# A one-core Mamba-2, attention and ConvFFN trunk: the low halves of the in-projection's weights are subtracted on GpSimd, and 22 small parameter loads are issued behind the first two of them

## The chip, the cores and the metric

The kernel runs on one core of a Trainium2 chip. The metric is the device time of one execution in microseconds; three runs of the kernel before gave a median of 1357.01 us. The core has five engines that take instructions from queues of their own, each in program order: TensorE (PE, matrix products; PEld is its loading of weights), VectorE (DVE), ScalarE (ACT), GpSimd (POOL) and SyncE (SP, here only the issuing of transfers). GpSimd and ScalarE can issue transfers too. Engines wait for each other through semaphores.

## The reference

For a sequence of 512 tokens of width 1024 (float32) the reference computes two layers. Only the first stage of the first layer matters here:

```python
def mamba2_mixer(x, ln_g, in_w, conv_w, conv_b, dt_bias, a_log, d_skip, norm_g, out_w):
    zxbcdt = rms_norm(x, ln_g) @ in_w
    z, xbc, dt = ...
    xbc = jax.nn.silu(causal_dwconv(xbc, conv_w, conv_b))
    ...
    dt = jax.nn.softplus(dt + dt_bias)
    a = dt * (-jnp.exp(a_log))
    y = ssd_chunked(xs32 * dt[..., None], a, bm, cm)
    y = y + xs32 * d_skip[:, None]
    y = y.reshape(b, s, D_INNER) * jax.nn.silu(z)
    y = rms_norm(y in 4 groups, norm_g)
    return y @ out_w
```

The in-projection `in_w` is 1024 wide on the input side and has 5152 columns: 2048 for `z`, 2048 for `x`, 512 for `B`, 512 for `C` and 32 for `dt`. After the mixer come a ConvFFN, a shared key/value projection, differential attention and a second ConvFFN.

## The kernel before, in words

**Products.** The stream is held transposed, 128 features on the partitions and 512 tokens along them. TensorE multiplies numbers of a shortened float32 type (fp32r). To keep float32 accuracy each operand is a sum of a high part (the value rounded to fp32r) and a low part (what is left over), and each product is three: high weights by high stream, high weights by low stream, low weights by high stream (`mm3`, lines 195 to 198). A block of 128 output columns of the in-projection takes 8 steps along its 1024 inputs, so 24 products of 128x512.

**Weights.** All weights pass in one order, the list `plan`: `dt` (32 columns), then for each of four groups one `B` block (`in32` to `in35`), one `C` block (`in36` to `in39`), four `x` blocks (`in16` and up) and four `z` blocks (`in0` and up), then the out-projection of the group before. Every entry is a chunk of 128x1024 numbers, 512 KB. The class `Weights` takes a chunk in three steps: SyncE loads it into one of three buffers `wr`; ScalarE copies it, rounded, into `wh` (`high`, line 147); VectorE subtracts `wh` from `wr` and writes `wl` (`low`, line 151). `wh` and `wl` have three buffers each. A chunk is taken two ahead of its use (`AHEAD`), so a `high` waits until the chunk three places earlier has been used up. There are 40 chunks of the in-projection. `in32` and `in36` (`c0`, `c1_`) are written out by hand ahead of the loop, 38 go through `split`.

**Start.** While the input is transposed and split into `xgh` and `xgl`, GpSimd issues the loads of all small parameters: first those needed soon, then 22 that are needed late (lines 259 to 272): `k_norm_g`, `q_norm_g`, `subln_g` and `lam_vecs` into the tile `s2t`, and 16 pieces of the ConvFFN's kernels and biases into `sf`. TensorE reads `s2t` through one transpose and `sf` through four (`pst`, line 235).

**The decay chain.** The first products give `dt` for all tokens. It is turned to lie along the tokens (`al_x`, line 456, and `ps_dtt`, line 550), then VectorE takes some twenty short steps on 128x128 numbers (`dt`, `sp_p`, `sp_s`, lines 558 to 577) up to `A`. TensorE sums `A` along a chunk of tokens (`ps_dec`, lines 581 to 583). The sums go out to memory and back, spread over the partitions (`cumd`, line 602; `m`, line 623; `er`, line 628; all issued by GpSimd), GpSimd sets what lies above the diagonal of `m` to minus infinity (line 633), ScalarE takes the exponential, and the scan's products (`st`, `y`, `yo`) use it. Between those steps VectorE runs the convolution of every `x`, `B` and `C` block (`ctmp`, line 535, three steps each), the `z` blocks' scaling and the scan's element-wise work.

**What orders the work.** Each engine's queue is filled by a scheduler that orders the instructions by their dependences and their expected length; a call inside `pin` is held in the order in which the program makes it. GpSimd has little to do: parameter loads, the transfers and selects of the scan, and a few sums of squares (`gacc`, line 785; `nacc`, line 499).

Of the kernel before, what the change touches and what calls it, by code (L numbers as in the profile page):

```python
# [18 lines left out]
P = 128  # L19
# [9 lines left out]
FFN = 2816  # L29
# [10 lines left out]
def trunk_kernel(ctx: ExitStack, tc, x, ssm_ln_g, ssm_in_w, ssm_conv_w, ssm_conv_b, ssm_dt_bias,  # L40
# [4 lines left out]
    act, dve, pool, pe, sync = nc.scalar, nc.vector, nc.gpsimd, nc.tensor, nc.sync  # L45
# [80 lines left out]
    pin = tc.keep_in_program_order  # L126

    class Weights:
# [17 lines left out]
            self.wl = wp.tile([P, 1024], F32R, tag="wl", name="wl_" + self.key)  # L146
            return act.activation(self.wh[:, :self.n], self.raw[:, :self.n], AF.Copy)  # L147

        def low(self):
            ready.append((self.key, self.cols(self.wh), self.cols(self.wl)))  # L150
            return dve.tensor_tensor(out=self.wl[:, :self.n], in0=self.raw[:, :self.n],  # L151
                                     in1=self.wh[:, :self.n].bitcast(F32), op=ALU.subtract)

        def split(self):
            if self.gcol is None:
                self.high()
                self.low()
                return

            wh = self.wh = wp.tile([P, 1024], F32R, tag="wh", name="wh_" + self.key)  # L160
            wl = self.wl = wp.tile([P, 1024], F32R, tag="wl", name="wl_" + self.key)
            for k in range(self.nk):
                ks = slice(k * self.ncol, (k + 1) * self.ncol)
                g = c2[:, self.gcol + k:self.gcol + k + 1]
                act.activation(wh[:, ks], self.raw[:, ks], AF.Copy, scale=g)
                dve.scalar_tensor_tensor(out=wl[:, ks], in0=self.raw[:, ks], scalar=g,
                                         in1=wh[:, ks].bitcast(F32), op0=ALU.mult, op1=ALU.subtract)
            ready.append((self.key, self.cols(wh), self.cols(wl)))
# [10 lines left out]
    pin = tc.keep_in_program_order  # L179
# [49 lines left out]
    sf = bp.tile([P, 4, P], F32, tag="nsq", name="sf", bufs=2)  # L229
    s2t = bp.tile([P, T], F32, tag="nsq", name="s2t", bufs=2)  # L230
    st2, lamv, d2 = s2t[:80, 0:P], s2t[:, P:3 * P].rearrange("p (a b) -> p a b", a=4), s2t[:, 384:386]
# [6 lines left out]
    with tc.tile_pool(name="ph0", bufs=1) as p0:  # L238
# [17 lines left out]
        pin(pool.dma_start(st2[16:32, :], ffn_ln_g.rearrange("o (b p) -> (o b) p", p=P)))  # L256
        pin(pool.dma_start(st2[32:40, :], kv_ln_g.rearrange("(b p) -> b p", p=P)))
        pin(pool.dma_start(st2[40:48, :], attn_ln_g.rearrange("o (b p) -> (o b) p", p=P)))
        for j in range(2):
            pin(pool.dma_start(st2[48:49, j * 64:(j + 1) * 64], k_norm_g.unsqueeze(0)))  # L260
            pin(pool.dma_start(st2[49:50, j * 64:(j + 1) * 64], q_norm_g))
        pin(pool.dma_start(st2[50:51, :], subln_g))
        pin(pool.dma_start(lamv.rearrange("p a b -> p (a b)"),
                       lam_vecs.rearrange("o a b -> (o a b)").partition_broadcast(P)))
        for l in range(2):
            for j in range(2):
                cols = slice(j * FFN, (j + 1) * FFN)
                d = sf[:, 2 * l + j, :]
                for t in range(3):
                    pin(pool.dma_start(d[22 * t:22 * (t + 1), :],  # L270
                                   ffn_conv_w[l, t, cols].rearrange("(b p) -> b p", p=P)))
                pin(pool.dma_start(d[66:88, :], ffn_conv_b[l, cols].rearrange("(b p) -> b p", p=P)))


        warm = aux_bank("warm")
        for _ in range(10):
# [36 lines left out]
        c0 = Weights(1)  # L313
        square(1)
        square(2)
        c1_ = Weights(2, xt[3])
        pss = [(mm_bank if k >= 4 else aux_bank)("xgt%d" % k) for k in range(6)]
        for b in range(NT):
            for k in range(6):
                turn(b, k)  # L320
        high(0)
        low(0)
        wdt = cdt.both()
        high(1)
        low(1)
        high(2)
        keep(0)
        keep(1)
        low(2)
        pss.extend(aux_bank("xgt%d" % k) for k in range(6, KB))  # L330
        ps_dt, ps_b0 = mm_bank("ps_dt"), mm_bank("ps_in32")
# [23 lines left out]
        for k in range(4, 6):  # L355
            high(k)
            low(k)
        pin(c0.low())
        for k in range(6, KB):
            high(k)  # L360
            low(k)
        pin(c1_.high())
        pin(c1_.low())
        state["next"], state["use"] = 3, 1
        square(3)
        for k in (4, 5, 2, 3, 6, 7):
# [150 lines left out]
    with tc.tile_pool(name="ssm_y", bufs=1) as yp, tc.tile_pool(name="ssm", bufs=1) as sp:  # L517
# [74 lines left out]
        ncum = sp.tile([P, P], F32, name="ncum")  # L592
        dve.tensor_scalar(out=ncum, in0=ps[:, P:2 * P], scalar1=-1.0, scalar2=None, op0=ALU.mult)
        dve.tensor_copy(rows(cum[:, 0, :]), split(ps[:, P:2 * P]))
        dve.tensor_copy(rows(cum[:, 1, :]), split(dec[:, P:2 * P]))
        ps = aux_bank("ps_cum")
        cumT = sp.tile([P, 2, P], F32, name="cumT")
# [611 lines left out]
```

## Time and profile before

| quantity | value |
|---|---|
| median of three runs (lowest, highest) | 1357.01 us (1356.84, 1357.68) |
| the profiled execution | 1357.51 us |
| its span in the profile | 1355.3 us |
| TensorE busy, instructions | 99%, 6421 |
| VectorE busy, instructions | 68%, 1527 |
| ScalarE busy, instructions | 48%, 1066 |
| GpSimd busy, instructions | 7%, 118 |
| granted TensorE clock | full in every slice |

The span runs from the first to the last instruction; 2.2 us of the execution lie around it. A row of a timeline gives the start (in us from the span's start), the duration, the engine, the line of the kernel, the operation, the tile that is written and those that are read, and in brackets how long the engine stood idle before and what ended that. Several alike in a row are one row with a count. A product's shown duration is longer than its distance to the next, since products overlap in the array; it is the distance that counts.

### The profile page before, as it was taken

The numbers are of one execution on the slowest core, as the hardware profiler recorded it, in microseconds if no ns is written. First come the engines' busy times: TensorE is split into PE (matmuls) and PEld (weight loads), VectorE is DVE, ScalarE is ACT, GpSimd is POOL, SyncE is SP. The second block draws the span as 40 slices with busy tenths as digits, with TensorE's granted clock in tenths as the row PEclk, the third lists the DMA queues.
The fourth block names the chain that finished last, engine by engine and source line by source line (L and its number), as shares of the span: only waits on it lengthen the run. The fifth ranks groups of instructions, "written<-read, shape, count | busy, mean of one in ns | idle before, by whom it ended". The sixth has DMA issues, their size and how long they took to land.

```text
span 1355.3 us, 16860 instructions
## 1 busy us (share of the span) xinstructions
PE 1348.1 (99%) x6421; PEld 1096.3 (81%) x6421; DVE 917.8 (68%) x1527; ACT 653.9 (48%) x1066; POOL 88.4 (7%) x118
## 2 busy tenths in 40 slices
PE   9999999999999999999999999999999999999998
PEld 7877887887888888888888777777888888888887
DVE  5989888688887774267754555778777773367742
ACT  5696744652444442234433556767654442134420
POOL 4230300200010000000001000000110000000000
PEclk9999999999999999999999999999999999999999
DMA  7452433532333333333323422221223333333322
GB/s 203 144 164 78 148 109 94 148 94 70 94 93 94 94 95 104 97 94 94 101 78 107 124 84 85 77 76 37 78 84 90 104 95 94 93 101 102 94 93 78
DMA packets 179904, 135.06 MB, mean 100 GB/s; under 512 B 6508, under 2 KB 163632, under 8 KB 179824
## 3 DMA queue, kind: packets, MB, share of 16 engines
q1 hardware_dynamic: 174048, 120.84, 30.0%
q0 software_dynamic: 4496, 12.05, 2.9%
q8 instruction: 50, 0.82, 0.3%
q10 hardware_dynamic: 1280, 1.10, 0.2%
q14 instruction: 30, 0.25, 0.1%
HBM read 131.72 MB, written 2.25 MB: 99 GB/s over the span
## 4 chain that ended last, share of the span: by engine, by line
PE 95%; DVE 3%; ACT 1%; issue 1%; DMA 0%; POOL 0%; SPq 0%; DVEq 0%; ACTq 0%
PE ps_g L197 6%; PE ps_g L198 6%; PE ps_g L196 6%; PE ps_u L198 6%; PE ps_u L196 6%; PE ps_u L197 6%; PE ps_in L197 5%; PE ps_in L196 5%; PE ps_in L198 5%; PE ps_d L854 3%; PE ps_d L198 3%; PE ps_d L197 3%; PE ps_d L853 3%; PE ps_d L852 3%; PE ps_d L196 3%; PE ps_o L196 2%
## 5 line engine op out<-in xcount | busy, mean ns | idle before, releaser
L196 PE MATMUL ps_u<-xgh,wh_u 128*128 128x512 f32 x352 | 137.4, 390 | 0.0
L197 PE MATMUL ps_g<-xgl,wh_g 128*128 128x512 f32 x352 | 137.2, 390 | 0.0
L196 PE MATMUL ps_g<-xgh,wh_g 128*128 128x512 f32 x352 | 137.0, 389 | 0.0
L198 PE MATMUL ps_u<-xgh,wl_u 128*128 128x512 f32 x352 | 137.0, 389 | 0.0
L198 PE MATMUL ps_g<-xgh,wl_g 128*128 128x512 f32 x352 | 137.0, 389 | 0.0
L197 PE MATMUL ps_u<-xgl,wh_u 128*128 128x512 f32 x352 | 136.9, 389 | 0.0
L197 PE MATMUL ps_in<-xgl,wh_in 128*128 128x512 f32 x304 | 120.9, 398 | 0.0
L196 PE MATMUL ps_in<-xgh,wh_in 128*128 128x512 f32 x304 | 120.9, 398 | 0.0
L151 DVE TENSOR_TENSOR wl_d<-wr_d,wh_d 128x1024 fp32r<-128x1024 f32 (+1 forms) x46 | 54.2, 1179 | 96.9 <-ACT wh_d L147 96.7
L198 PE MATMUL ps_in<-xgh,wl_in 128*128 128x512 f32 x304 | 119.6, 393 | 0.0
L147 ACT ACTIVATE wh_d<-wr_d 128x1024 fp32r<-128x1024 f32 (+1 forms) x46 | 47.1, 1024 | 130.6 <-PE ps_d L854 62.4
L876 ACT ACTIVATE hh<-vg 128x512 fp32r<-128x512 f32 x44 | 27.8, 632 | 114.9 <-DVE vg L875 114.9
L824 DVE TENSOR_TENSOR uu<-ps_u,nr_f 128x512 f32<-128x512 f32 x44 | 30.4, 692 | 78.0 <-PE ps_u L198 77.8
L197 PEld LDWEIGHTS ps_g<-xgl,wh_g 128*128 128x128 f32 x352 | 66.1, 188 | 14.5 <-DVE xgl L414 0.7
L198 PEld LDWEIGHTS ps_u<-xgh,wl_u 128*128 128x128 f32 x352 | 66.0, 188 | 13.8
L196 PEld LDWEIGHTS ps_u<-xgh,wh_u 128*128 128x128 f32 x352 | 66.2, 188 | 13.5
L198 PEld LDWEIGHTS ps_g<-xgh,wl_g 128*128 128x128 f32 x352 | 66.1, 188 | 13.5
L197 PEld LDWEIGHTS ps_u<-xgl,wh_u 128*128 128x128 f32 x352 | 66.0, 188 | 13.6
L196 PEld LDWEIGHTS ps_g<-xgh,wh_g 128*128 128x128 f32 x352 | 66.0, 187 | 13.6
L147 ACT ACTIVATE wh_g<-wr_g 128x1024 fp32r<-128x1024 f32 x44 | 46.7, 1061 | 50.5 <-PE ps_u L197 32.2
L196 PE MATMUL ps_d<-hh,wh_d 128*128 128x512 f32 x176 | 68.5, 389 | 0.0
L197 PE MATMUL ps_d<-hl,wh_d 128*128 128x512 f32 x176 | 68.5, 389 | 0.0
(347 smaller groups left out, 3178.3 us busy)
## 6 DMA issues: line engine op xcount, KB each, us to landing
wr_g<-in_ffn_up_w_dram SPq DMA_DIRECT2D x44, 512.0 KB, 3.8
wr_u<-in_ffn_up_w_dram SPq DMA_DIRECT2D x44, 512.0 KB, 3.8
wr_d<-in_ffn_down_w_dram SPq DMA_DIRECT2D x42, 512.0 KB, 3.6
wr_in<-in_ssm_in_w_dram SPq DMA_DIRECT2D x40, 512.0 KB, 3.9
m<-cumd POOLq DMA_DIRECT2D x16, 512.0 KB, 4.5
wr_out<-in_ssm_out_w_dram SPq DMA_DIRECT2D x16, 512.0 KB, 3.5
wr_k<-in_kv_w_dram SPq DMA_DIRECT2D x8, 512.0 KB, 3.8
wr_q<-in_q_w_dram SPq DMA_DIRECT2D x8, 512.0 KB, 3.8
```

Of the source, the lines that this page charges most:

```text
L147: return act.activation(self.wh[:, :self.n], self.raw[:, :self.n], AF.Copy)
L151: return dve.tensor_tensor(out=self.wl[:, :self.n], in0=self.raw[:, :self.n], in1=self.wh[:, :self.n].bitcast(F32), op=ALU.subtract)
L196: pe.matmul(ps, wh, xh, start=start, stop=False)
L197: pe.matmul(ps, wh, xl, start=False, stop=False)
L198: return pe.matmul(ps, wl, xh, start=False, stop=stop).ins
L824: dve.tensor_tensor(out=u, in0=ps, in1=r, op=ALU.mult)
L852: pe.matmul(pss[b], hh[k][:, ts], wh[:, k - k0, :], start=k == 0, stop=False)
L853: pe.matmul(pss[b], hh[k][:, ts], wl[:, k - k0, :], start=False, stop=False)
L854: pe.matmul(pss[b], hl[k][:, ts], wh[:, k - k0, :], start=False, stop=k == n - 1)
L876: act.activation(h, ga, AF.Copy)
```

## The change

`low` takes the engine as an argument. The low parts of all 40 chunks of the in-projection, 128x1024 each, are subtracted on GpSimd; those of all other weights stay on VectorE. The 22 late parameter loads move from their place ahead of the first products to a place behind the low part of `in36`.

```diff
-        def low(self):
+        def low(self, eng=dve):
             ready.append((self.key, self.cols(self.wh), self.cols(self.wl)))
-            return dve.tensor_tensor(out=self.wl[:, :self.n], in0=self.raw[:, :self.n],
+            return eng.tensor_tensor(out=self.wl[:, :self.n], in0=self.raw[:, :self.n],
                                      in1=self.wh[:, :self.n].bitcast(F32), op=ALU.subtract)
         def split(self):
             if self.gcol is None:
                 self.high()
-                self.low()
+                self.low(pool if self.key[:2] == "in" else dve)
                 return
...
         pin(pool.dma_start(st2[40:48, :], attn_ln_g.rearrange("o (b p) -> (o b) p", p=P)))
-        for j in range(2):
-            pin(pool.dma_start(st2[48:49, j * 64:(j + 1) * 64], k_norm_g.unsqueeze(0)))
...
-                pin(pool.dma_start(d[66:88, :], ffn_conv_b[l, cols].rearrange("(b p) -> b p", p=P)))
...
-        pin(c0.low())
+        pin(c0.low(pool))
         for k in range(6, KB):
             high(k)
             low(k)
         pin(c1_.high())
-        pin(c1_.low())
+        pin(c1_.low(pool))
+        for j in range(2):
+            pin(pool.dma_start(st2[48:49, j * 64:(j + 1) * 64], k_norm_g.unsqueeze(0)))
...
+                pin(pool.dma_start(d[66:88, :], ffn_conv_b[l, cols].rearrange("(b p) -> b p", p=P)))
```

The 14 lines that move are the same in both places. What GpSimd's queue holds behind the last of these loads, before the change (a name's first part is the tile, `x3` means three alike in a row):

```order
L270 DMA sf_112<-in_ffn_conv_w_dram 22x128 x3
L272 DMA sf_112<-in_ffn_conv_b_dram 22x128
L602 DMA cumd0_417<-cumT_416 128x128
L602 DMA cumd1_418<-cumT_416 128x128
L623 DMA m0_0_429<-cumd0_417 128x1024
```

And after it, at the same place of GpSimd's queue:

```order
L360 DMA sf_112<-in_ffn_conv_w_dram 22x128 x3
L362 DMA sf_112<-in_ffn_conv_b_dram 22x128
L151 TENSOR_TENSOR wl_in16_449<-wr_in16_446,wh_in16_448 128x1024
L151 TENSOR_TENSOR wl_in17_463<-wr_in17_460,wh_in17_462 128x1024
L151 TENSOR_TENSOR wl_in18_483<-wr_in18_480,wh_in18_482 128x1024
L151 TENSOR_TENSOR wl_in19_522<-wr_in19_519,wh_in19_521 128x1024
L151 TENSOR_TENSOR wl_in0_572<-wr_in0_569,wh_in0_571 128x1024
L151 TENSOR_TENSOR wl_in1_622<-wr_in1_619,wh_in1_621 128x1024
L601 DMA cumd0_417<-cumT_416 128x128
L601 DMA cumd1_418<-cumT_416 128x128
L622 DMA m0_0_429<-cumd0_417 128x1024
```

Six subtractions, of the four `x` blocks and the first two `z` blocks of group 0, now stand between the late loads and the transfers of the decay chain. The subtractions of `in2` and `in3` follow behind the four selects of group 0, those of the later groups in the same way.

Since the scheduler orders what is not pinned, TensorE's queue changes as well. Before, the block `in16` begins in the usual pattern of three, right behind the transpose of `st1`, the last instruction of the hand-written start:

```order
L383 MATMUL pst_339<-ident_77,st1_122 128x120
L196 MATMUL ps_in16_486<-xgh0_86,wh_in16_448 128x512
L197 MATMUL ps_in16_486<-xgl0_94,wh_in16_448 128x512
L198 MATMUL ps_in16_486<-xgh0_86,wl_in16_449 128x512
L196 MATMUL ps_in16_486<-xgh1_87,wh_in16_448 128x512
L197 MATMUL ps_in16_486<-xgl1_95,wh_in16_448 128x512
```

After the change:

```order
L382 MATMUL pst_339<-ident_77,st1_122 128x120
L196 MATMUL ps_in16_486<-xgh0_86,wh_in16_448 128x512
L197 MATMUL ps_in16_486<-xgl0_94,wh_in16_448 128x512
L196 MATMUL ps_in17_525<-xgh0_86,wh_in17_462 128x512
L197 MATMUL ps_in17_525<-xgl0_94,wh_in17_462 128x512
L455 MATMUL al_x_364<-ident_77,rs_84 128x128 x4
L549 MATMUL ps_dtt_372<-ident_77,dtT_370 128x64 x4
L198 MATMUL ps_in16_486<-xgh0_86,wl_in16_449 128x512
L196 MATMUL ps_in16_486<-xgh1_87,wh_in16_448 128x512
```

Two products of `in17` and the eight transposes of `al_x` and `ps_dtt` now stand ahead of the first product that reads the low part of `in16`. The three products of `ps_dec` move as well. Before, they stand in the block `in19`:

```order
L197 MATMUL ps_in19_625<-xgl5_99,wh_in19_521 128x512
L581 MATMUL ps_dec_404<-A_401,lt_81 128x128
L582 MATMUL ps_dec_404<-A_401,ut_79 128x128
L583 MATMUL ps_dec_404<-A_401,ones_75 128x128
L198 MATMUL ps_in19_625<-xgh5_91,wl_in19_522 128x512
```

After it they stand in `in18`, at the same step of the block:

```order
L197 MATMUL ps_in18_575<-xgl5_99,wh_in18_482 128x512
L580 MATMUL ps_dec_404<-A_401,lt_81 128x128
L581 MATMUL ps_dec_404<-A_401,ut_79 128x128
L582 MATMUL ps_dec_404<-A_401,ones_75 128x128
L198 MATMUL ps_in18_575<-xgh5_91,wl_in18_483 128x512
```

That is one block of 24 products earlier. The scan's products of group 0 that follow stand earlier by about as much.

More of the change, by code (lines that the diff above doesn't have):

```diff
@@ L258, in trunk_kernel @@
         pin(pool.dma_start(st2[40:48, :], attn_ln_g.rearrange("o (b p) -> (o b) p", p=P)))
-        for j in range(2):
[L260 to L272, printed above, removed]
         warm = aux_bank("warm")
@@ L362, in trunk_kernel @@
         pin(c1_.high())
-        pin(c1_.low())
+        pin(c1_.low(pool))
+        for j in range(2):
+            pin(pool.dma_start(st2[48:49, j * 64:(j + 1) * 64], k_norm_g.unsqueeze(0)))
+            pin(pool.dma_start(st2[49:50, j * 64:(j + 1) * 64], q_norm_g))
+        pin(pool.dma_start(st2[50:51, :], subln_g))
+        pin(pool.dma_start(lamv.rearrange("p a b -> p (a b)"),
+                       lam_vecs.rearrange("o a b -> (o a b)").partition_broadcast(P)))
+        for l in range(2):
+            for j in range(2):
+                cols = slice(j * FFN, (j + 1) * FFN)
+                d = sf[:, 2 * l + j, :]
+                for t in range(3):
+                    pin(pool.dma_start(d[22 * t:22 * (t + 1), :],
+                                   ffn_conv_w[l, t, cols].rearrange("(b p) -> b p", p=P)))
+                pin(pool.dma_start(d[66:88, :], ffn_conv_b[l, cols].rearrange("(b p) -> b p", p=P)))
         state["next"], state["use"] = 3, 1
```

## The prediction

> **What bounds the kernel now.** I read the page's busy times first, then the chain that ended last, then TensorE's waits.
>
> ```profile
> PE 1348.1 (99%) x6421; PEld 1096.3 (81%) x6421; DVE 917.8 (68%) x1527; ACT 653.9 (48%) x1066; POOL 88.4 (7%) x118
> PE 95%; DVE 3%; ACT 1%; issue 1%; DMA 0%; POOL 0%; SPq 0%; DVEq 0%; ACTq 0%
> ```
>
> TensorE carries the chain. Its waits (waiting line, releaser: total us, count, longest) say how little another engine could give back:
>
> ```profile
> PE warm L277 <- DVE ones L202: 1.1, 1, 1.1
> PE tr_g L446 <- DVE gacc L785: 0.4, 1, 0.4
> PE at L1050 <- DVE lg L1042: 0.4, 1, 0.4
> PE st L675 <- DVE xe L658: 0.3, 1, 0.3
> ```
>
> Behind the warm-up nothing waits longer than 0.4 us. VectorE's relief, however large, can buy about 0.7 us (`tr_g` and `st`) where it is relieved. The relief is 48.9 us of work that nothing waited for (the group's row is below), so the question is whether TensorE gets new waits. A product costs what lies between two starts:
>
> ```profile
> 27.32 0.39 PE L197 MATMUL ps_in<-xgl,wh_in 128*128 128x512 f32 x1
> 27.55 0.40 PE L198 MATMUL ps_in<-xgh,wl_in 128*128 128x512 f32 x1
> ...
> 31.06 0.62 PE L456 MATMUL al_x<-ident,rs 128*128 128x128 f32 x4
> 31.61 0.46 PE L550 MATMUL ps_dtt<-ident,dtT 64*128 64x64 f32 x4
> 32.00 0.50 PE L197 MATMUL ps_in<-xgl,wh_in 128*128 128x512 f32 x1
> ```
>
> 27.55 - 27.32 = 0.23 us a 512-wide product; `al_x` and `ps_dtt` together take 32.00 - 31.06 = 0.94. The row at 27.55 is the first product that reads the low part of `in16`.
>
> **What one subtraction costs on GpSimd.** The first row is the group that leaves VectorE; GpSimd subtracts nothing so far, and the nearest rows are its 512-wide additions, with VectorE's 512-wide addition as the last row:
>
> ```profile
> L151 DVE TENSOR_TENSOR wl_in<-wr_in,wh_in 128x1024 fp32r<-128x1024 f32 x40 | 48.9, 1223 | 3.8 <-ACT wh_in L147 3.8
> 369.15 1.29 POOL L499 TENSOR_TENSOR nacc_f<-nacc_f,nsq_f 128x512 f32<-128x512 f32 x1 [30.55 <-ACT nsq_f L497]
> 373.01 1.30 POOL L499 TENSOR_TENSOR nacc_f<-nacc_f,nsq_f 128x512 f32<-128x512 f32 x1 [2.57 <-ACT nsq_f L497]
> 369.12 1.87 DVE L414 SCALAR_TENSOR_TENSOR xgl<-xT,c,xgh 128x512 fp32r<-128x512 f32 x1
> ...
> 373.05 0.68 DVE L511 TENSOR_TENSOR xT<-ps_o,xT 128x512 f32<-128x512 f32 x1
> ```
>
> Twice 1.29 gives 2.58; scaled as VectorE scales, 1.29 x 1.22 / 0.68, it is 2.3. I take 2.4. The loads behind it and the next step of GpSimd's queue:
>
> ```profile
> 11.71 0.50 POOL L260 DMA_DIRECT2D s2t<-in_k_norm_g_dram  x1
> ...
> 25.06 0.51 POOL L272 DMA_DIRECT2D sf<-in_ffn_conv_b_dram  x1
> 53.47 0.57 POOL L602 DMA_DIRECT2D cumd<-cumT  x1 [27.91 <-issue]
> ...
> 68.06 1.09 POOL L633 TENSOR_SCALAR_AFFINE_SELECT m<-m 128x1024 f32<-128x1024 f32 x1 [2.74 <-DMA m<-cumd]
> ```
>
> The 22 issues took 25.57 - 11.71 = 13.9 us with their pauses, and need at least 22 x 0.51 = 11.2.
>
> **The first two blocks: free.** ScalarE's high part of `in36`, and the first products that read the low parts of `in32` and `in36`:
>
> ```profile
> 15.36 1.12 ACT L147 ACTIVATE wh_in<-wr_in 128x1024 fp32r<-128x1024 f32 x1
> 19.72 1.98 PE L375 MATMUL ps_in<-xgh,wl_in 128*128 128x512 f32 x8
> 21.99 0.39 PE L381 MATMUL ps_in<-xgh,wl_in 128*128 128x512 f32 x1
> ```
>
> On GpSimd `in36` is done at 15.36 + 1.12 + 2.4 = 18.9, three us before its use, and `in32`, whose high part came earlier, by 17.8. The moved parameters are issued by 32.8 at the latest (term 1) and are first read within the decay chain, some microseconds behind that, so their own lateness costs nothing; reloading the raw buffers stays hidden too, since a block of 24 products lasts 24 x 0.23 = 5.5 us.
>
> **Term 1, `in16`.** Its subtraction now stands behind the 22 issues: from 18.9 they last until 30.1 (11.2) to 32.8 (13.9). I take 31.0, towards the lower end, because the rows of the single issues are the nearest to what is asked; plus 2.4 gives 33.4 (32.5 to 35.3). Nothing else on GpSimd is late by that: what is queued behind are the other subtractions, whose blocks come later. TensorE reaches its first use two products of `in17` and the transposes later than before: 27.55 + 2 x 0.23 + 0.94 = 28.95. The wait is 4.5 us (3.5 to 6.3). Part of it would come anyway, since `al_x` needs `rs`:
>
> ```profile
> 28.04 1.23 DVE L151 TENSOR_TENSOR wl_in<-wr_in,wh_in 128x1024 fp32r<-128x1024 f32 x1
> ...
> 30.75 0.16 DVE L429 SCALAR_TENSOR_TENSOR rs<-rst_x,rs 128x4 f32<-128x4 f32 x1
> 32.10 0.29 DVE L558 COPY dt<-ps_dtt 128x128 f32<-128x128 f32 x1 [1.20 <-PE ps_dtt L550]
> ...
> 48.00 0.28 DVE L577 SCALAR_TENSOR_TENSOR A<-dt,alog 128x128 f32<-128x128 f32 x1
> ```
>
> `rs` was ready at 30.91; without the subtraction in its midst it is at 29.8, against 28.0 for TensorE at `al_x`. That is 1.8 us, inside the 4.5.
>
> **Term 2, `ps_dec`.** It stands one block earlier:
>
> ```profile
> 48.68 0.39 PE L581 MATMUL ps_dec<-A,lt 128*128 128x128 f32 x2
> 65.69 0.39 PE L198 MATMUL ps_in<-xgh,wl_in 128*128 128x512 f32 x1
> L535 DVE SCALAR_TENSOR_TENSOR ctmp<-u,c,ctmp 128x511 f32<-128x511 f32 x24 | 17.7, 743 | 0.0
> ```
>
> TensorE comes there 61 products behind the first use of `in16`'s low part: 33.4 + 61 x 0.23 = 47.4. VectorE's chain to `A` took 48.28 - 32.10 = 16.2 us. Two subtractions (2.4) and one convolution step (0.74) fall out of it: 13.0. It starts at 29.8 + 0.94 = 30.7, so `A` is there at 43.7, in time, if VectorE runs as fast as before. But the rows at 369 show that it doesn't: beside GpSimd's addition `xgl` took 1.87 us, against 0.74 of the alike step in the `L535` row, so it stood for 1.13 of GpSimd's 1.29, 88%. The addition out of PSUM at 373.05 was not slowed. Five subtractions (`in16` to `in0`) fall into this chain: 12.0 us, less some 2.4 in which VectorE reads PSUM, times 0.88, is 8.4. `A` then comes at 52.1, and TensorE waits 4.7 us (0 to 5.9). It is an estimate from one pair of rows; the chain's steps have two inputs outside PSUM, as `xgl` had, so I take that row.
>
> The Trainium skill, page "GPSIMD Engine Reference", section "8. Key points", says that GpSimd shares its SBUF interfaces with VectorE and contends with VectorE's instructions that have two SBUF inputs. For `xgl` the trace agrees, with 1.87 against 0.74; for convolution steps no run here shows it. By that rule term 2 stays as it is; without it, it would be nought.
>
> **Term 3, `in2`.** Its subtraction stands behind the transfers and selects of group 0. `A` at 52.1 would put the first of these transfers at 52.1 + (53.47 - 48.28) = 57.3. Ahead of it on GpSimd now stands the subtraction of `in1`, whose high part waits until `in18` is used up: 52.1 + 0.4 for `ps_dec` + 7 x 0.23 + 1.1 (a high part) + 2.4 = 57.6, which decides by a little. The last select follows 14.6 us later as before, at 72.2; with its 1.1 and 2.4 more, the low part is there at 75.7. TensorE needs it at 65.69 before; less 0.94 and 0.46 that have moved ahead of `in16` and 0.3 of a moved scan product, 36.4 us behind `in16`'s first use: 33.4 + 36.4 + 4.7 = 74.5. The wait is 1.2 (0 to 3).
>
> **Term 4, groups 1 to 3.** There 30 subtractions meet a VectorE that is in places full:
>
> ```profile
> 120.00:150.00 30.00, 30.00 (x183) 23.09 (x182) 29.35 (x47) 17.03 (x31) 4.80 (x7) 1.00 0.40 127
> ```
>
> (The window, its length, then the busy time of PE, PEld, DVE, ACT and POOL with counts, TensorE's granted clock and the transfers' share and rate.) VectorE is busy for 29.35 of 30 us in the scan, whose order has changed. For each subtraction of 1.22 that it loses it can stand for up to 2.1 (0.88 x 2.4), so it comes out up to 0.9 later for each, and behind it are queued the scan's steps on which TensorE's `st`, `y` and `yo` wait. GpSimd itself, busy for 4.80 of the 30, has room for these. I take 1.5 us over three groups (-0.7, the relief above, to 5).
>
> **Sum.** 4.5 + 4.7 + 1.2 + 1.5 = 11.9. The profiled run took 1357.51, 1355.3 of it the span; the median is 1357.01, and the terms are differences, so I add them to the median: 1368.9.
>
> **Rivals.**
>
> *The port doesn't bite the chain (A).* For: only one kind of step was seen slowed, and a 128x128 step may slip between. Against: 88% at `xgl`. Then term 2 is gone and term 3 with it, and 4.5 + 1.5 + some 1 for a partly slowed chain makes 1364. Chance 0.20.
>
> *TensorE's clock falls in the pauses (C).* The warm-up shows what a cold clock costs:
>
> ```profile
> 1.13 4.63 PE L277 MATMUL warm<-ones 128*128 128x128 f32 x20 [1.13 <-DVE ones L202]
> ...
> 9.40 1.28 PE L344 MATMUL ps_in<-ones 128*128 128x128 f32 x10
> ```
>
> 4.63 / 20 = 0.23 a product at the start, 1.28 / 10 = 0.13 later: about half speed, for between 4.6 us (the first row alone) and 8.3 (until the second). Half of that is lost, 2.3 to 4.1 a fall. No pause of before is long enough to show whether 4.5 us suffice. One or both pauses falling add about 3: 1371.9. Chance 0.19.
>
> The Trainium skill, page "TensorE: Matmul & The Clock Gate", Part 1, says that one idle window of about 3.4 us halves the clock and that about 3.4 busy us restore it. By that figure a fall would lose an estimated 1.7 us, and the forecast with two falls would be 1372.3; no run here shows a fall within the kernel.
>
> *Not slower (B).* This needs the late loads off `in16`'s way: all 22 issued by 28.95 - 2.4 = 26.5, in 7.6 us instead of 11.2, that is at 0.35 each or on fewer instructions than the order shows, and the port free. Then the pause on `rs`, 1.8, less the relief, 0.7, is left: 1358.1. Nothing in the rows speaks for issues that short. Chance 0.06.
>
> **How the numbers follow.** The forecast has the remaining 0.55. Its bounds with small terms (3.5 + 1 + 0) and A reach down to 1361; C with term 1 at its upper end and two or three us more in the later groups reaches 1377. That leaves out B and little at either end, some 0.15. A measurement of this kernel tells about 0.2%, 2.7 us, from no change: faster by more 0.01, within 0.05 (B), slower 0.94.
>
> **What would show it.** Term 1: GpSimd's 22 issues in one row until about 31, `wl_in16` until 33, TensorE's longest wait on it, near 4.5 us. Term 2: a wait of `ps_dec` on `A`, and convolution steps well over 0.74 us wherever a subtraction runs. Term 3: a small wait in `in2`. C: slower products behind a pause, or a granted clock under 1. I am wrong if the `in16` wait is under 2 us, if the steps of the decay chain keep their 0.28 us beside GpSimd, or if a later group holds a wait larger than these.

## The result and the profile after

Five runs of the changed kernel gave a median of 1403.95 us (1399.96 to 1405.26), beside 1357.01 of the kernel before on the same chip: a ratio of 1.0339 (95% interval 1.0327 to 1.0351), 46.9 us slower, where 11.9 us were forecast. The profiled execution took 1403.95 us, with a span of 1402.2.

The page of the changed kernel, busy times:

```profile
PE 1359.3 (97%) x6421; PEld 1103.8 (79%) x6421; DVE 925.6 (66%) x1487; ACT 659.7 (47%) x1070; POOL 187.2 (13%) x158
```

VectorE has lost 40 subtractions, 48.9 us of work, and is busy for 925.6 us, 7.8 more than before. The other 1487 instructions are the same in both kernels, tile by tile, and their rows add up to 47.9 us more than before: an instruction that cannot get at its data counts as busy, and stands. (The busy time counts overlapping rows once, so the two busy times don't give this figure.) Of the 47.9, 24.2 us lie in the three convolution steps. The group of the first of them, which had a mean of 743 ns:

```profile
L534 DVE SCALAR_TENSOR_TENSOR ctmp<-u,c,ctmp 128x511 f32<-128x511 f32 x24 | 31.7, 1320 | 15.4 <-ACT ctmp L532 15.4
```

TensorE's waits, which before had nothing over 0.4 us behind the warm-up:

```profile
PE xs L652 <- ACT xs L536: 13.4, 3, 4.7
PE al_x L455 <- DVE rs L428: 8.5, 1, 8.5
PE yo L669 <- DVE S L680: 4.5, 1, 4.5
PE ps_dec L580 <- DVE A L576: 2.6, 1, 2.6
PE yo L669 <- ACT bt L661: 2.5, 3, 0.9
PE ps_in L198 <- POOL wl_in L151: 1.7, 1, 1.7
PE al_g L455 <- DVE tr_g L428: 1.5, 1, 1.5
```

Together 34.7 us, and 0.9 more in a row further down (`dtT`); some 11 of the 46.9 are left. They fit the slower products behind the longer pauses: TensorE is busy for 22.8 us at a granted clock of 0.50, and half of that is lost, 11.4. Of the waits shown only one, of 1.7 us, is for a subtraction on GpSimd. All others are for VectorE or ScalarE.

**The first pause.** VectorE's steps of `rs` and GpSimd's queue at the same time:

```profile
29.05 0.16 DVE L426 TENSOR_TENSOR rst_x<-rs 128x4 f32<-128x4 f32 x1
29.25 7.84 DVE L427 SCALAR_TENSOR_TENSOR rst_x<-rst_x,rsm_x 128x4 f32<-128x4 f32 x1
37.13 0.16 DVE L428 SCALAR_TENSOR_TENSOR rs<-rst_x,rs 128x4 f32<-128x4 f32 x1
```

```profile
19.13 0.53 POOL L350 DMA_DIRECT2D s2t<-in_k_norm_g_dram  x1
...
30.12 6.95 POOL L151 TENSOR_TENSOR wl_in<-wr_in,wh_in 128x1024 fp32r<-128x1024 f32 x3
```

The 22 issues took 30.12 - 19.13 = 11.0 us and the subtractions 2.3 to 2.4 each, both as forecast. But a step that takes 0.16 us stood for 7.84, until all three subtractions were through. Its row begins 0.87 us before that of the first subtraction, while GpSimd issues its last two loads; what held it there already is not shown, since the steps just before it took 0.16 beside the same issues. On TensorE:

```profile
37.94 1.12 PE L455 MATMUL al_x<-ident,rs 128*128 128x128 f32 x4 [8.46 <-DVE rs L428]
...
40.19 0.63 PE L196 MATMUL ps_in<-xgh,wh_in 128*128 128x512 f32 x1
40.62 0.63 PE L197 MATMUL ps_in<-xgl,wh_in 128*128 128x512 f32 x1
...
42.55 0.39 PE L196 MATMUL ps_in<-xgh,wh_in 128*128 128x512 f32 x1
42.78 0.39 PE L197 MATMUL ps_in<-xgl,wh_in 128*128 128x512 f32 x1
```

`al_x` waits for `rs`. Behind the pause products are 0.43 us apart (40.62 - 40.19) and later 0.23 again (42.78 - 42.55). The windows behind this pause, behind the 2.6 us before `ps_dec` and behind one of the 4.4 us before `xs` (window, length, busy times, then the granted clock):

```profile
37.90:42.50 4.60, 4.56 (x15) 3.55 (x16) 2.79 (x8) 2.23 (x3) 0.00 (x0) 0.52 0.48 130
57.60:62.00 4.40, 4.37 (x22) 3.54 (x23) 3.58 (x8) 4.34 (x5) 0.85 (x1) 1.00 0.20 57
249.20:254.00 4.80, 4.73 (x17) 4.11 (x18) 3.32 (x3) 2.10 (x5) 2.37 (x1) 0.51 0.10 22
```

The clock was halved behind the first and the third, not behind the second.

**The pause of each later group.** One `x` block of group 2 on VectorE, ScalarE and GpSimd:

```profile
242.18 0.69 DVE L529 TENSOR_TENSOR u<-ps_in,nr_x 128x512 f32<-128x512 f32 x1
244.68 3.81 DVE L534 SCALAR_TENSOR_TENSOR ctmp<-u,c,ctmp 128x511 f32<-128x511 f32 x3 [1.81 <-ACT ctmp L532]
248.41 0.69 DVE L529 TENSOR_TENSOR u<-ps_in,nr_x 128x512 f32<-128x512 f32 x1
```

```profile
242.36 0.63 ACT L536 ACTIVATE xs<-ctmp 128x512 f32<-128x512 f32 x1 [3.98 <-DVE ctmp L534]
242.90 1.04 ACT L147 ACTIVATE wh_in<-wr_in 128x1024 fp32r<-128x1024 f32 x1
243.84 0.80 ACT L532 ACTIVATE ctmp<-u,c 128x512 f32<-128x512 f32 x1
```

```profile
244.02 2.35 POOL L151 TENSOR_TENSOR wl_in<-wr_in,wh_in 128x1024 fp32r<-128x1024 f32 x1 [3.87 <-ACT wh_in L147]
```

Here is a loop. The convolution of one block ends; ScalarE takes its SiLU, then the high part of a chunk, then the first convolution step (`ctmp`) of the next block. The end of that high part starts GpSimd's subtraction (244.02), and 0.66 us later VectorE wants its three steps (244.68). They take 3.81 instead of 2.32. From `u` to `u` it is 248.41 - 242.18 = 6.23 us, more than the 5.44 in which TensorE brings a block (24 products, 0.227 us apart). In group 2 of the kernel before, the four distances from the `u` of the `C` block on are 3.79, 5.44, 5.44 and 5.44 us; in the change they are 6.81, 4.37, 6.26 and 6.23. So VectorE falls behind by about 2 us up to the second `x` block, where a step of the `C` block stood for 2.77 us (at 228.86), and by 0.8 us with each block after it. How much room there had been is in a row of the kernel before:

```profile
211.61 0.63 ACT L537 ACTIVATE xs<-ctmp 128x512 f32<-128x512 f32 x1 [2.88 <-DVE ctmp L535]
```

```profile
212.43 0.49 PE L653 MATMUL xs<-ident,xs 128*128 128x128 f32 x3
```

The SiLU ended at 212.24, and TensorE started the three transposes of this row at 212.43, 212.54 and 212.65. The third is the one that waits after the change. Nothing waited, with 0.2 to 0.4 us to spare.

**The pause in the scan of group 0.** A step of the state `S` that takes 0.69 us, and what GpSimd did:

```profile
96.76 4.25 DVE L679 TENSOR_TENSOR S<-S,dec 128x512 f32<-128x512 f32 x1
```

```profile
97.03 1.11 POOL L632 TENSOR_SCALAR_AFFINE_SELECT m<-m 128x1024 f32<-128x1024 f32 x1
98.09 2.35 POOL L151 TENSOR_TENSOR wl_in<-wr_in,wh_in 128x1024 fp32r<-128x1024 f32 x1
```

The step stands through the select and the subtraction. The subtraction is one of group 1's; the step that it holds up belongs to group 0.

### The profile page after: what moved, and what is told of

It is laid out like the page before. It is cut to its first block, busy times and chain, and to the rows that moved or that the text cites. A ratio compares the mean times of both kernels' runs of the same rounds, so it can differ in the third digit from the quotient of the medians.

```text
span 1402.2 us, 16864 instructions
## 1 busy us (share of the span) xinstructions
PE 1359.3 (97%) x6421; PEld 1103.8 (79%) x6421; DVE 925.6 (66%) x1487; ACT 659.7 (47%) x1070; POOL 187.2 (13%) x158
## 3 DMA queue, kind: packets, MB, share of 16 engines
q1 hardware_dynamic: 174048, 120.84, 29.1%
## 4 chain that ended last, share of the span: by engine, by line
PE 71%; DVE 2%; ACT 1%; issue 0%; DVEq 0%; ACTq 0%
PE ps_g L197 6%; PE ps_g L196 6%; PE ps_g L198 6%; PE ps_u L196 5%; PE ps_u L197 5%; PE ps_u L198 5%; PE ps_d L851 3%; PE ps_d L198 3%; PE ps_d L852 3%; PE ps_d L196 3%; PE ps_d L197 3%; PE ps_d L853 3%; PE lg L1014 1%; PE po L1060 1%; PE ps_k L933 1%; PE ps_k L932 1%
## 5 line engine op out<-in xcount | busy, mean ns | idle before, releaser
L196 PE MATMUL ps_in<-xgh,wh_in 128*128 128x512 f32 x304 | 124.0, 408 | 0.9 <-ACT dtT L545 0.9
L151 POOL TENSOR_TENSOR wl_in<-wr_in,wh_in 128x1024 fp32r<-128x1024 f32 x40 | 97.5, 2444 | 148.9 <-ACT wh_in L147 148.5
L534 DVE SCALAR_TENSOR_TENSOR ctmp<-u,c,ctmp 128x511 f32<-128x511 f32 (+2 forms) x72 | 77.9, 1082 | 16.5 <-ACT ctmp L532 15.4
L196 PEld LDWEIGHTS ps_u<-xgh,wh_u 128*128 128x128 f32 x352 | 66.1, 188 | 13.5
L197 PEld LDWEIGHTS ps_u<-xgl,wh_u 128*128 128x128 f32 x352 | 66.0, 188 | 13.5
L147 ACT ACTIVATE wh_g<-wr_g 128x1024 fp32r<-128x1024 f32 x44 | 46.7, 1062 | 51.9 <-PE ps_u L197 32.5
```

The costliest lines, as they stand in the source:

```text
L151: return eng.tensor_tensor(out=self.wl[:, :self.n], in0=self.raw[:, :self.n], in1=self.wh[:, :self.n].bitcast(F32), op=ALU.subtract)
L196: pe.matmul(ps, wh, xh, start=start, stop=False)
L197: pe.matmul(ps, wh, xl, start=False, stop=False)
L534: dve.scalar_tensor_tensor(out=tmp[:, s:], in0=u[:, :T - s], scalar=w(3 - s), in1=tmp[:, s:], op0=ALU.mult, op1=ALU.add)
```

## The experiments

Theory 1 is that VectorE stands still while GpSimd works in the on-chip memory. Its rivals are that the late loads (2) or the new order of the queues (3) make the waits. Every kernel is compared with the kernel before as it ran beside it (a median of 1357.40, 1356.70 or 1356.79 us).

**The loads alone.**

```diff
-                self.low(pool if self.key[:2] == "in" else dve)
+                self.low()
...
-        pin(c0.low(pool))
+        pin(c0.low())
...
-        pin(c1_.low(pool))
+        pin(c1_.low())
```

> The 22 late loads stand behind the first two blocks as in the change, but all 40 subtractions stay on VectorE; every engine's order is that of the kernel before, but for the place of the loads on GpSimd. Theory 1 (VectorE stands still while GpSimd subtracts): nothing stands still, 1357, within 2 us. Theory 2 (the loads, issued later, are what is late): clearly above 1357, by up to the 9 us that TensorE waited for rs and the transposes.

1357.29 us, a ratio of 0.9999 (0.9989 to 1.0008). The late loads cost nothing by themselves; theory 2 falls.

**The first two blocks and the loads.**

```diff
-                self.low(pool if self.key[:2] == "in" else dve)
+                self.low()
```

> The loads moved and only the subtractions of in32 and in36 on GpSimd; the other 38 on VectorE, and the order of TensorE and ScalarE as before. Theory 1: two subtractions beside a VectorE that reads PSUM at that time; 1357, within 2 us. Theory 2: as in the run with the loads alone, above 1357.

1357.28 us, 0.9999 (0.9989 to 1.0008). This part of the change is free, as forecast, and nothing is won by it either: TensorE wasn't waiting there.

**The other 38 subtractions, the loads at their old place** (the kernel before with the changed `low` and `split`).

```diff
-        def low(self):
+        def low(self, eng=dve):
...
-                self.low()
+                self.low(pool if self.key[:2] == "in" else dve)
```

> The other half: 38 subtractions on GpSimd, those of in32 and in36 on VectorE, the loads at their old place ahead of all. Theory 1: three subtractions still run in a row near 26 to 33 us, over the steps of rs, and the waits of all four groups stay; 1390 to 1405. Theory 2: without the late loads the wait on rs and half of what follows go; 1357 to 1385.

1404.71 us, 1.0348 (1.0330 to 1.0365): the whole loss. VectorE's first step of `rs` and GpSimd's queue:

```profile
28.14 4.28 DVE L421 TENSOR_SCALAR rsm_x<-rs 128x4 f32<-128x4 f32 x1
```

```profile
25.34 7.04 POOL L151 TENSOR_TENSOR wl_in<-wr_in,wh_in 128x1024 fp32r<-128x1024 f32 x3
```

The step stands until the row of three has ended (25.34 + 7.04 = 32.38). `al_x` waits 4.5 us here instead of 8.5, and other waits make up for it.

**Subtractions that nobody reads.** The kernel before, with VectorE's work unchanged and its order nearly so:

```diff
+        state["spare"] = sp.tile([P, 864], F32, name="spare")
...
         def low(self):
             ready.append((self.key, self.cols(self.wh), self.cols(self.wl)))
+            if "spare" in state and self.key[:2] == "in":
+                pool.tensor_tensor(out=state["spare"], in0=self.raw[:, :864], in1=self.wh[:, :864].bitcast(F32), op=ALU.subtract)
```

> The kernel before, with all its subtractions on VectorE, and beside it 38 subtractions on GpSimd of 128x864 from the same two tiles into a tile that nobody reads; TensorE's order is that of before but for a few products. Nothing waits for these results, so only what GpSimd does to the other engines by running is measured. Theory 1: VectorE, which keeps its own 47 us of subtractions, stands still for most of 38 x 2.0 us and TensorE waits for it in every group; 1380 to 1420. Theory 3 (the waits come from the new order of TensorE's and ScalarE's queues, not from the port): 1357 to 1362.

1399.53 us, 1.0308 (1.0292 to 1.0323). TensorE's longest waits:

```profile
PE xs L657 <- ACT xs L541: 10.3, 3, 4.8
PE al_x L458 <- DVE rs L431: 5.5, 1, 5.5
PE al_g L458 <- DVE tr_g L431: 4.9, 3, 3.6
PE ps_dec L585 <- DVE A L581: 3.9, 1, 3.9
```

They stand at places of the change's waits, and no result of these subtractions is waited for. They also hold the buffers `wr` longer, but ScalarE hardly notices: it waits 2.4 us in all for transfers of these chunks, 2.1 in the kernel before. So GpSimd's running is enough for a loss of 42.1 us, and theory 3, that the new order makes the waits, isn't needed for one of this size. What share it has within the change this run can't say: VectorE still does its own subtractions here, and the loss is spread otherwise, with 13.5 us up to the last product of group 0, where the change has lost 26.0.

**The same in quarters.**

```diff
-                pool.tensor_tensor(out=state["spare"], in0=self.raw[:, :864], in1=self.wh[:, :864].bitcast(F32), op=ALU.subtract)
+                for q in range(4):
+                    qs = slice(q * 216, (q + 1) * 216)
+                    pool.tensor_tensor(out=state["spare"][:, qs], in0=self.raw[:, qs],
+                                       in1=self.wh[:, qs].bitcast(F32), op=ALU.subtract)
```

> As the run with subtractions that nobody reads (1399.5), but each of them cut into four instructions of 128x216, so the same numbers pass through GpSimd in shorter instructions. Theory 1a (an instruction of GpSimd keeps VectorE out until it ends, and VectorE gets its turn between two): a step of VectorE stands for at most some 0.6 us instead of 2 and more; TensorE's pauses mostly go, 1360 to 1378. Theory 1b (GpSimd keeps VectorE out for as long as instructions are queued in a row, as the 7.8 us of one small step suggest): as before the cut, 1392 to 1404.

1393.54 us, 1.0268 (1.0253 to 1.0284): the time of 1b, but the rows show the mechanism of 1a. VectorE beside a row of twelve quarters, the first of which starts at 27.55:

```profile
30.50 0.60 DVE L432 TENSOR_TENSOR rst_x<-rs 128x4 f32<-128x4 f32 x1
31.13 0.56 DVE L433 SCALAR_TENSOR_TENSOR rst_x<-rst_x,rsm_x 128x4 f32<-128x4 f32 x1
```

VectorE gets its turn after each quarter, but every step then waits for the next one: 0.56 instead of 0.16, step after step, and `al_x` waits 5.0 us. A chain of short steps pays per step; shorter instructions on GpSimd help little, 36.8 us lost instead of 42.1.

**Fills instead of subtractions.**

```diff
-                pool.tensor_tensor(out=state["spare"], in0=self.raw[:, :864], in1=self.wh[:, :864].bitcast(F32), op=ALU.subtract)
+                pool.memset(state["spare"], 0.0)
```

> The kernel before with 38 fills of a 128x864 tile that nobody reads on GpSimd, in place of the subtractions; since they wait for nothing, 31 of them stand in a row behind the parameter loads, over the steps of rs and the decay chain. They read nothing. Theory 1c (what GpSimd reads keeps VectorE out): no step stands, 1357, within 2 us. Theory 1d (every access of GpSimd does): the steps of rs near 28 us stand as long as with the subtractions, TensorE waits 4 us and more for them, 1362 to 1385.

1358.17 us, 1.0010 (1.0000 to 1.0019). Neither expectation is whole. GpSimd fills without a pause from 27.49 to 54.69 (31 fills, 0.82 us for one). On VectorE:

```profile
28.37 0.84 DVE L424 TENSOR_SCALAR rs<-rsm_x 128x4 int32<-128x4 int32 x1
...
30.47 0.16 DVE L429 TENSOR_TENSOR rst_x<-rs 128x4 f32<-128x4 f32 x1
...
35.23 0.75 DVE L539 SCALAR_TENSOR_TENSOR ctmp<-u,c,ctmp 128x511 f32<-128x511 f32 x1
```

Steps with two inputs pass at full speed beside a GpSimd that only writes; a step with one input (0.17 us otherwise) stands for a whole fill. The Trainium skill, page "SBUF — State Buffer", section "Who interferes with whom", says that VectorE's instructions with two inputs there contend with GpSimd's instructions that read, not with those that only write. It says too that copies and `tensor_scalar` can run in a mode that takes both of the ports there and then contend with GpSimd, and that whoever issues first has the shared ports for its whole instruction while the other blocks. The trace agrees: 0.16 and 0.75 us beside fills with two inputs, 0.84 with one, the length of one fill. The step that stood 4.28 us above is more than that, since it stood through the rest of one subtraction and the whole of the next.

**Group 0 alone, and groups 1 to 3 alone.**

```diff
-                self.low(pool if self.key[:2] == "in" else dve)
+                self.low(pool if self.key in ("in16", "in17", "in18", "in19", "in0", "in1", "in2", "in3") else dve)
```

> The change with GpSimd's subtractions in the first two blocks and group 0 alone; the 30 of groups 1 to 3 on VectorE. Theory 1 with places that add up: the waits of the first 120 us stay (rs 8.5, dtT 0.9, A 2.6, in2 1.7, S 4.5) and some 5 us of slower products behind them; 1357 + 23 = 1380, within 3. Rival (a delay of group 0 is what makes the waits of the later groups): nearly the whole loss, over 1390.

```diff
-                self.low(pool if self.key[:2] == "in" else dve)
+                self.low(pool if self.key[:2] == "in" and self.key not in ("in16", "in17", "in18", "in19", "in0", "in1", "in2", "in3") else dve)
```

> The other part: GpSimd's subtractions in the first two blocks and groups 1 to 3, those of group 0 on VectorE. Theory 1 with places that add up: three times a wait of xs (4.4 to 4.7) and of yo (0.8), al_g 1.5, and some 2 us of slower products a group; 1357 + 23 = 1380, within 3. Rival: without a late group 0 the later groups catch up, under 1368.

1373.79 us (1.0124, 1.0109 to 1.0139) and 1385.82 us (1.0208, 1.0191 to 1.0225): 17.1 and 29.1 us, 46.2 together, against 46.9 for the change. They add up, but not as 23 and 23. The wait for `S`, which I had counted in group 0, is gone in the first kernel, since the subtraction beside it was group 1's (the rows at 97 us), and in the second group 1 loses 17.3 us instead of 6.1. This table gives how much later than in the kernel before TensorE starts the last product of a stage (the 144th, 240th, 480th, 720th and 960th of the in-projection in each timeline, 24 a block; before: 50.73, 84.51, 156.86, 247.67 and 338.48 us):

| kernel | group 0, `x` | group 0 | group 1 | group 2 | group 3 |
|---|---|---|---|---|---|
| the change | 15.1 | 26.0 | 32.1 | 39.7 | 47.5 |
| group 0 alone | 15.3 | 18.7 | 16.9 | 16.9 | 16.9 |
| groups 1 to 3 alone | 0.1 | 0.0 | 17.3 | 25.5 | 33.7 |
| without `in16` to `in18` | 8.9 | 10.5 | 28.0 | 36.1 | 44.2 |
| only the 15 beside the convolution | 0.0 | 0.2 | 12.3 | 18.1 | 25.1 |
| only the 17 outside of it | -0.1 | 7.3 | 10.3 | 12.5 | 14.6 |

(The profiled executions of the third and the last kernel took 1390.4 and 1370.9 us, the longest and the shortest of their runs.) Groups 2 and 3 lose 7.6 and 7.8 us each in the change, and nothing where their subtractions stay on VectorE.

**The first three of group 0 back on VectorE.**

```diff
-                self.low(pool if self.key[:2] == "in" else dve)
+                self.low(pool if self.key[:2] == "in" and self.key not in ("in16", "in17", "in18") else dve)
```

> The change with the three subtractions that ran in a row over the steps of rs (in16, in17, in18) back on VectorE. Theory 1 with places that add up: the wait on rs (8.5) and the 2.1 of slow products behind it go, the others stay; 1404 - 10.6 = 1393, within 3. Rival (what is saved there is waited for at ps_dec): 1400 or more.

1400.05 us, 1.0318 (1.0301 to 1.0335): the rival. The wait on `rs` is gone, and the next one has grown:

```profile
PE xs L652 <- ACT xs L536: 13.0, 3, 4.4
PE ps_dec L580 <- DVE A L576: 5.9, 1, 5.9
```

TensorE reaches `ps_dec` earlier and waits 5.9 us there instead of 2.6; of the 6.2 us saved up to the end of `in19` (15.1 - 8.9), 3.3 are left at the end.

**Which subtractions of a group cost.** The 17 that fall outside of the `x` blocks' convolution, and the other 15 of groups 1 to 3:

```diff
+    BESIDE = ("in2", "in3", "in33", "in37", "in20", "in6", "in7", "in34", "in38", "in24", "in10", "in11", "in35", "in39", "in28", "in14", "in15")
...
-                self.low(pool if self.key[:2] == "in" else dve)
+                self.low(pool if self.key in BESIDE else dve)
```

> GpSimd subtracts the first two blocks and only those 17 chunks whose subtraction falls outside of the three convolution steps of an x block: in2 and in3, and in each of groups 1 to 3 the B block, the C block, the first x block and the last two z blocks. The others are on VectorE. Theory 4 (in groups 1 to 3 the loss is a loop: a subtraction starts when ScalarE's high part ends, just when the convolution of the block before starts, and makes ScalarE and VectorE need 6.2 us a block, more than TensorE's 5.45): no wait on xs over 1 us; 1357 to 1370. Rival 4b (each subtraction costs about the same, 29.1 / 30 = 1.0 us): 1357 + 17 = 1374, within 3.

```diff
+    AGAINST = ("in21", "in22", "in23", "in4", "in5", "in25", "in26", "in27", "in8", "in9", "in29", "in30", "in31", "in12", "in13")
...
-                self.low(pool if self.key in BESIDE else dve)
+                self.low(pool if self.key in AGAINST else dve)
```

> The complement in groups 1 to 3: GpSimd subtracts the first two blocks and the 15 chunks whose subtraction falls beside the convolution steps of an x block (the last three x blocks and the first two z blocks of each group). Theory 4: the waits on xs stay as they are, some 4.4 us a group and 2 us of slow products behind each; 1357 + 3 x 6.5 = 1376 to 1386. Rival 4b: 1357 + 15 = 1372 or less.

1373.13 us (1.0117, 1.0102 to 1.0132) and 1381.99 us (1.0185, 1.0170 to 1.0200). The second is theory 4's. The first has theory 4's sign in the waits, no wait on `xs` above 0.9 us, but 4b's time. Its waits:

```profile
PE ps_in L199 <- POOL wl_in L152: 3.4, 1, 3.4
PE tr_g L446 <- DVE gacc L785: 3.0, 1, 3.0
PE xs L653 <- ACT xs L537: 2.5, 3, 0.9
```

The two largest lie at 67 to 70 us (`in2`, whose subtraction stands behind the selects, the place of term 3) and at 100 to 103 us, in and behind the scan of group 0; by the table 10.3 of its us are lost by the end of group 1. In groups 2 and 3 these subtractions cost 2.1 us a group and the 15 others 5.8 and 7.0, of 7.6 and 7.8 in the change. The distances from `u` to `u` in group 2 agree: with the 17 they are 3.79, 5.44, 5.44 and 5.44 us as in the kernel before, with the 15 they are 6.81, 4.37, 6.26 and 6.23 as in the change. So the loop is shown there as the main part. That each subtraction costs the same is not: the 15 cost 25.2 us, and the 17 cost 16.3, most of it in group 0 and right behind its end.

## Why the prediction was wrong

The direction and the resource were right, the size was not, by a factor of four. Terms 1 to 3 gave group 0 a loss of 10.4 us, and it lost 26.0; term 4 gave groups 1 to 3 a loss of 1.5, and they lost 21.5. Two of the signs of being wrong came: no wait on `in16`, and waits of 4.4 to 4.7 us in the later groups.

**Right.** 2.4 us for a subtraction on GpSimd (mean 2.44); 11.0 us for the 22 issues and `wl_in16` at 32.5 (31.0 and 33.4 were forecast for the end of the issues and of the subtraction); the first two blocks free; VectorE standing beside GpSimd, also in convolution steps, which rival A denied. `in2`, forecast at 1.2 us and measured at 1.7, has the right cause, but its size is partly luck: its low part was to be there at 75.7 and came at 82.3, and TensorE came at 80.6 instead of 74.5.

**Term 1, the step that named the wrong wait.** "The wait is 4.5 us" was to be for `in16`'s low part; this was there before TensorE came for it. TensorE stood 8.5 us at `al_x`, for `rs`, from 29.48 on; with `rs` in time it would have stood about 2 us for `in16` instead (32.5 against 29.48 + 0.94). I had worked out that `rs` would be ready at 29.8 us, with VectorE's own subtraction gone, and applied the standing still, which I priced under term 2, only to the chain behind `ps_dtt`. The three subtractions that the loads hold back start just then, in a row.

**Term 2** was forecast at 4.7 and is 2.6. In the run without the three it is 5.9: its size depends on how late TensorE already is. The 4.5 us at `S`, also in group 0, stood in no term.

**Term 4, the mis-sized term.** "I take 1.5 us over three groups", with 5 as the most; measured are 47.5 - 26.0 = 21.5. I weighed the standing of each subtraction (2.1) against its relief (1.22), as if it were a matter of load. The loss is one of order: each subtraction starts when the high part ends, that is, when the convolution of a block is about to start, and the loop over ScalarE and VectorE becomes longer than TensorE's block. This is shown for groups 2 and 3. How the loss of group 1 comes about, 6.1 us here and 17.3 with group 0 on VectorE, was not separated. All parts of the loop stood in the trace of before: 0.63 for the SiLU, 1.06 for the high part, 0.80 for `ctmp`, 2.32 for the convolution, 4.8 in all; with 1.5 of standing still it is 6.3, against 5.44. And a list of waits doesn't show the slack, which was 0.2 to 0.4 us at the `xs` transposes.

**Rival C** was not a rival but came on top: the clock fell to 0.50 in or behind the five longest pauses (4.4 to 8.5 us), and the products behind them lost 1.7 to 2.6 us each, 11.4 in all, where 2.3 to 4.1 a fall were priced. The Trainium skill, page "TensorE: Matmul & The Clock Gate", Part 1, puts the idle window at about 3.4 us. In the changed kernel that agrees (0.52 behind 8.5 us, 1.00 behind 2.6). In the run with subtractions that nobody reads it doesn't quite: there a pause of 2.3 us sufficed. So the length of a pause alone doesn't decide: the clock was 0.50 over the 3 us behind a pause of 2.5 us (groups 1 to 3 alone, at 134.81), and 1.00 behind one of 3.0 us (the 17, at 103.28). The windows of the run with subtractions that nobody reads, in that pause and behind it:

```profile
102.70:105.06 2.36, 0.05 (x1) 0.00 (x0) 2.36 (x7) 1.16 (x6) 2.36 (x3) 0.98 0.59 171
105.06:108.20 3.14, 3.14 (x9) 2.47 (x10) 3.14 (x6) 2.96 (x12) 2.44 (x5) 0.50 0.65 180
```

**What stays open.** How much of the 46.9 us the new order of TensorE's queue adds was not separated from the standing still. Nor was it tried to keep the clock up in the pauses.

## What to carry to other kernels

Work moved from VectorE to GpSimd isn't gone from VectorE while both work in the on-chip memory: here 48.9 us taken away came back as 47.9 us of standing still, much of it in chains that TensorE then waited for. Before moving it, ask which instruction of VectorE will run at that very moment, and add up the loop that goes through it, since a sum of busy times and a list of waits show neither the collision nor how little slack a hidden chain has. A pause of TensorE can cost more than its length: here the clock was halved in or behind every pause of 3.4 us or more, and some of 2.3 to 3.2.

## What the runs showed of the hardware

A step of VectorE can stand through several instructions of GpSimd: 0.16 us of work stood 7.84 us, through three subtractions of 2.35 to 2.37 us that started 2.30 us apart, and 4.28 us in the run with the loads at their old place. Beside the quarters, and beside the subtractions of 128x864 that nobody reads, it got its turn after each (2.07, 1.88 and 1.96 us for three of its steps). What decides between the two was not tried.

Which of VectorE's steps stand depends on where their inputs lie and on what GpSimd does. Those that read PSUM, the memory that TensorE writes to, did not stand (`u` took 0.68 to 0.69 us beside subtractions as elsewhere); those with two inputs outside of it stood beside subtractions (a convolution step up to 2.95 us instead of 0.75) and selects (`S` 1.52 us instead of 0.69, in the kernel before), not beside fills; a copy and a `tensor_scalar` with one input stood beside fills as well (0.84 us, one fill).

In the changed kernel TensorE's clock was halved for 3.41, 6.83 or 10.24 us at a time, once, twice or three times the same length.
